# The final norm of a two-layer decoder trunk: its sum of squares by a full block of ones

## The chip, the cores and the metric

The kernel runs on one core of one Trainium2 chip. The metric is the device time of one execution in microseconds (us), as the median of three runs. TensorE (PE) multiplies matrices, VectorE (DVE), ScalarE (ACT) and GpSimd (POOL) work element by element, and SyncE (SP) issues most transfers. Each engine carries out its own instructions in a fixed order and waits on semaphores for the others.

## The reference

Two decoder layers over 512 tokens of width 1024: sparse attention and a dilated sliding window, each with heads into 256 memory tokens, and after each a SwiGLU of width 2816. The change touches only what comes last, the final norm:

```
def rms_norm(x, g):
    xf = x.astype(jnp.float32)
    y = xf * lax.rsqrt(jnp.mean(xf * xf, axis=-1, keepdims=True) + EPS)
    return (y * g.astype(jnp.float32)).astype(x.dtype)
...
    x = x + swiglu_ffn(rms_norm(x, norm_ffn), w_gate_up, w_down)
...
return rms_norm(x, final_norm)
```

## The kernel before, in words

The state x is kept transposed, as xT: eight tiles of 128 channels (partitions) by 512 tokens (columns). A sum over the channels of a token is thus a sum over partitions and over the eight tiles. Large products are done with weights and activations split into a high and a low float32r part, three matmuls for each; the norm's own small matmuls are plain float32, and each of those shows in the trace as two passes of weight load and matmul.

The last stage is `final`. It is called by `ffn(1)` for the last of the eight output tiles of the down projection (`down`, whose matmuls stand on lines 222 to 224 of `mm3`). By then tiles 0 to 6 of xT are done, and GpSimd adds up their squares in the tile `ssq` (`parts[0]`). ScalarE makes `xg`, the same tiles times the gains. The last tile is done in two halves of 256 tokens. For each half TensorE does 22 x 3 matmuls into one bank `psS`; VectorE adds the sum to xT (L1263), ScalarE squares the result into `t` (L1264), and `norm` finishes these 256 tokens.

`norm` sums the squares over partitions: for each block of 128 tokens a matmul has the squares as the stationary side and two columns of ones as the moving side, first with `ssq` (L1224), then with the square of the last tile (L1226). The result has tokens on partitions, one number each. ScalarE takes the root (L1227), VectorE the reciprocal (L1228), both of a single column. VectorE multiplies an identity matrix by that column (L1229), and a matmul of ones with these two diagonal blocks (L1232) spreads the numbers as a row over all partitions, into the bank `psacc`. ScalarE copies the row to SBUF (L1234), since GpSimd is given the copy; then six products on VectorE read `psacc` (L1241, L1243) and two on GpSimd the copy (L1239), and four transfers of two tiles each bring the output out (L1248). In the second half these go in turn by SyncE's and ScalarE's queues.

`norm` is a generator. For the first half it is created when its squares are; it runs up to its `yield` behind the first four of the 22 input tiles of the second half's down projection, and the rest behind the next four. TensorE carries out its instructions in the order in which the program issues them, so the first half's small matmuls stand between those of the second half's projection; the order of the other engines is set by the scheduler. For the second half nothing follows, and `norm` runs to its end.

Of the kernel before, what the change touches and what calls it, by code (L numbers as in the profile page):

```python
# [12 lines left out]
AF = mybir.ActivationFunctionType  # L13
ALU = mybir.AluOpType
AX = mybir.AxisListType

D = 1024
# [47 lines left out]
class _Trunk:  # L65
# [1137 lines left out]
    def final(self, ws, mh, ml):  # L1203

        nc, mm = self.nc, self.nc.tensor.matmul
        n = S // 2
        last = KT - 1
        add, parts = self.squares()
        for k in range(last):
            add(self.xT[:, k], 0, nc.gpsimd)  # L1210
        eps = self.cst.tile([128, 1], F32, name="eps")
        nc.vector.memset(eps, EPS)
        bigs = [self.big(name, F32).rearrange("p (k n) -> p k n", k=4) for name in ("xg", "xg", "y", "y")]
        xg, y = ([bigs[2 * a + k // 4][:, k % 4] for k in range(KT)] for a in range(2))
        for k in range(last):
            nc.scalar.activation(xg[k], self.xT[:, k], AF.Copy, scale=self.gains[:, 6, k:k + 1])

        def norm(b, sq):

            r, d = self.col("root", 2), self.tmp("raw")[:, :n]  # L1220
            blocks = [slice(i * 128, (i + 1) * 128) for i in range(2)]
            q = [self.psum("T")[:, :2] for _ in range(2)]
            for i in range(2):
                mm(q[i], parts[0][:, b][:, blocks[i]], self.ones[:, :2], start=True, stop=False)  # L1224
            for i in range(2):
                mm(q[i], sq[:, blocks[i]], self.ones[:, :2], start=False, stop=True)  # L1226
                nc.scalar.activation(r[:, i:i + 1], q[i][:, :1], AF.Sqrt, scale=1.0 / D, bias=eps)  # L1227
                nc.vector.reciprocal(r[:, i:i + 1], r[:, i:i + 1])  # L1228
                nc.vector.tensor_scalar(d[:, blocks[i]], self.ident, r[:, i:i + 1], None, op0=ALU.mult)  # L1229
            yield  # L1230
            p = self.psum("acc")[:, :n]
            mm(p, self.ones, d, start=True, stop=True)  # L1232
            row = self.tmp("raw")[:, :n]
            nc.scalar.copy(row, p)  # L1234
            done = set()
            for k in self.OUT_ORDER:
                o = y[k][:, b]
                if k in self.POOL_TILES:
                    nc.gpsimd.tensor_tensor(out=o, in0=xg[k][:, b], in1=row, op=ALU.mult)  # L1239
                elif k < last:  # L1240
                    nc.vector.tensor_tensor(out=o, in0=xg[k][:, b], in1=p, op=ALU.mult)  # L1241
                else:
                    nc.vector.scalar_tensor_tensor(o, self.xT[:, k, b], self.gains[:, 6, k:k + 1], p, op0=ALU.mult,  # L1243
                                                   op1=ALU.mult)
                done.add(k)
                j = k // 2 * 2
                if k ^ 1 in done:
                    (nc.sync, nc.scalar)[k // 2 % 2 * (b.start > 0)].dma_start(out[:, j:j + 2, b], bigs[2 + j // 4][:, j % 4:j % 4 + 2, b])  # L1248

        out = self.io["out"].rearrange("(k p) n -> p k n", p=128)  # L1250
        job = iter(())
        for h in range(2):
            b = slice(h * n, (h + 1) * n)
            p = self.psum("S")[:, :n]
            for w, k0, k1 in ws:
                for k in range(k0, k1, 4):
                    e = min(k + 4, k1)
                    c = slice((k - k0) * 128, (e - k0) * 128)
                    self.down(p, [m[:, c] for m in w], k, e, [m[:, b] for m in mh], [m[:, b] for m in ml])
                    next(job, None)  # L1260
            sq = self.tmp("t")[:, :n]
            with self.tc.high_priority():
                nc.vector.tensor_tensor(out=self.xT[:, last, b], in0=self.xT[:, last, b], in1=p, op=ALU.add)  # L1263
                nc.scalar.activation(sq, self.xT[:, last, b], AF.Square)  # L1264
            job = norm(b, sq)
        for _ in job:
            pass
# [116 lines left out]
```

## Time and profile before

| | us |
|---|---|
| median of three runs | 1240.79 |
| lowest and highest of them | 1238.21 and 1242.46 |
| the profiled execution | 1237.89 |
| its span, first to last instruction | 1236.0 |
| TensorE busy in it | 1196.5 |
| VectorE, ScalarE, GpSimd busy in it | 529.3, 484.1, 350.2 |

The span is what the trace covers; the profiled execution's time has 1.89 us more around it. Every row further down is of this one execution, and its times count from the start of the span. The final norm takes place in the last 18 us of it.

### The profile page before, as it was taken

The page shows a single profiled execution, that of the slowest core. Times are in us where ns is not written, and L with a number is a line of the kernel's source. Part 1 is how long each engine was busy: PE and PEld are TensorE (multiplying, and loading weights), DVE is VectorE, ACT ScalarE, POOL GpSimd, SP SyncE. Part 2 cuts the span into 40 slices and gives each one's busy share as a digit, 9 for nine tenths or more (in the row PEclk, how much of TensorE's full clock was granted, in tenths as well). Part 3 has the DMA queues.
Part 4 walks back from the last instruction along what each step waited for, and adds up shares of the span by engine and source line. Part 5 has one row for each costly group of instructions (what it writes and reads, how often), then busy time and mean ns, then how long its engine had stood idle before and what let it go on. Part 6 is the DMA issues. An engine that isn't in the chain of part 4 may idle for free.

```text
span 1236.0 us, 14342 instructions
## 1 busy us (share of the span) xinstructions
PE 1196.5 (97%) x5624; PEld 944.8 (76%) x5624; DVE 529.3 (43%) x1022; ACT 484.1 (39%) x852; POOL 350.2 (28%) x220
## 2 busy tenths in 40 slices
PE   9799899999999999999999999998999999999997
PEld 5367576578788888888888778886788888888886
DVE  4769724547433333332224543559433333331112
ACT  3663584424423323222222776545323223222222
POOL 0444453245222122212222323324322122211222
PEclk9899999999999999999999999999999999999999
DMA  5313103102322222222233121211222222222221
GB/s 189 130 38 132 57 35 95 59 34 92 110 76 99 102 102 103 79 96 94 94 115 113 58 69 34 83 55 69 91 82 100 103 103 101 77 87 94 94 94 69
DMA packets 29185, 108.36 MB, mean 88 GB/s; under 512 B 2494, under 2 KB 11582, under 8 KB 20670
## 3 DMA queue, kind: packets, MB, share of 16 engines
q1 hardware_dynamic: 28574, 106.93, 24.6%
q8 instruction: 44, 0.72, 0.2%
q10 hardware_dynamic: 544, 0.52, 0.1%
q14 instruction: 23, 0.19, 0.0%
HBM read 104.43 MB, written 3.01 MB: 87 GB/s over the span
## 4 chain that ended last, share of the span: by engine, by line
PE 77%; DVE 10%; DMA 4%; issue 4%; ACT 3%; POOL 2%; SPq 0%; DVEq 0%; POOLq 0%; ACTq 0%
PE psS L249 5%; PE psS L247 5%; PE psS L248 5%; PE psT L249 3%; PE psT L247 3%; PE psT L248 3%; PE psacc L249 3%; PE psacc L247 3%; PE psacc L248 3%; PE psacc L222 3%; PE psacc L224 3%; PE psacc L223 3%; PE psS L222 3%; PE psS L224 3%; PE psS L223 3%
## 5 line engine op out<-in xcount | busy, mean ns | idle before, releaser
L51 POOL TENSOR_TENSOR wl<-wf,wh 128x1024 fp32r<-128x1024 f32 x92 | 222.7, 2422 | 618.9 <-ACT wh L48 567.4
L48 ACT CAST wh<-wf 128x1024 fp32r<-128x1024 f32 (+1 forms) x163 | 167.4, 1030 | 505.4 <-issue 156.1
L51 DVE TENSOR_TENSOR wl<-wf,wh 128x1024 fp32r<-128x1024 f32 (+1 forms) x84 | 99.4, 1184 | 80.0 <-ACT wh L48 80.0
L249 PE MATMUL psS<-xh,wl 128*128 128x512 f32 x272 | 106.9, 393 | 0.0
L247 PE MATMUL psS<-xh,wh 128*128 128x512 f32 x272 | 106.5, 392 | 0.0
L248 PE MATMUL psS<-xl,wh 128*128 128x512 f32 x272 | 106.1, 390 | 0.0
L247 PE MATMUL psacc<-xh,wh 128*128 128x512 f32 x192 | 75.5, 393 | 0.6 <-DVE xT L653 0.6
L247 PE MATMUL psT<-xh,wh 128*128 128x512 f32 x192 | 75.5, 393 | 0.0
L249 PE MATMUL psT<-xh,wl 128*128 128x512 f32 x192 | 75.5, 393 | 0.0
L249 PE MATMUL psacc<-xh,wl 128*128 128x512 f32 x192 | 75.5, 393 | 0.0
L248 PE MATMUL psT<-xl,wh 128*128 128x512 f32 x192 | 74.9, 390 | 0.0
L248 PE MATMUL psacc<-xl,wh 128*128 128x512 f32 x192 | 74.9, 390 | 0.0
L316 POOL TENSOR_TENSOR ssq<-ssq,t 128x512 f32<-128x512 f32 (+1 forms) x31 | 41.0, 1322 | 96.6 <-ACT t L306 61.1
L248 PEld LDWEIGHTS psS<-xl,wh 128*128 128x128 f32 x272 | 51.1, 188 | 11.6
L249 PEld LDWEIGHTS psS<-xh,wl 128*128 128x128 f32 x272 | 51.1, 188 | 11.1
L247 PEld LDWEIGHTS psS<-xh,wh 128*128 128x128 f32 x272 | 51.1, 188 | 10.7
L235 PE MATMUL psacc<-xh,wh 128*128 128x512 f32 x136 | 58.1, 428 | 0.0
L668 DVE TENSOR_TENSOR raw<-psacc,R 128x512 f32<-128x512 f32 x22 | 15.2, 691 | 96.9 <-PE psacc L249 96.9
L237 PE MATMUL psacc<-xh,wl 128*128 128x512 f32 x136 | 54.1, 398 | 0.0
L236 PE MATMUL psacc<-xl,wh 128*128 128x512 f32 x136 | 54.0, 397 | 0.0
L653 DVE TENSOR_TENSOR xT<-xT,psacc 128x512 f32<-128x512 f32 x44 | 30.0, 683 | 39.0 <-PE psacc L224 38.9
L247 PEld LDWEIGHTS psacc<-xh,wh 128*128 128x128 f32 x192 | 36.1, 188 | 8.7 <-issue 1.2
(320 smaller groups left out, 2628.8 us busy)
## 6 DMA issues: line engine op xcount, KB each, us to landing
wf<-in_gu SPq DMA_DIRECT2D x44, 1024.0 KB
wf<-in_dn SPq DMA_DIRECT2D x16, 1024.0 KB
wf<-in_in SPq DMA_DIRECT2D x12, 1024.0 KB
wf<-in_dn SPq DMA_DIRECT2D x16, 384.0 KB
wf<-in_v SPq DMA_DIRECT2D x3, 1024.0 KB
wf<-in_in SPq DMA_DIRECT2D x5, 512.0 KB
xT<-in_x SPq DMA_DIRECT2D x8, 256.0 KB
wf<-in_mk SPq DMA_DIRECT2D x2, 1024.0 KB
```

The lines of the kernel that those rows point to most:

```text
L48: nc.scalar.copy(hi, src)
L51: lo_engine.tensor_tensor(out=lo, in0=src, in1=hi.bitcast(F32), op=ALU.subtract)
L222: mm(out, wh[k], xh[k], start=first and k == 0, stop=False)
L223: mm(out, wh[k], xl[k], start=False, stop=False)
L224: mm(out, wl[k], xh[k], start=False, stop=last and k == n - 1)
L235: mm(out, wh[:, s], xh[k], start=k == 0, stop=False)
L236: mm(out, wh[:, s], xl[k], start=False, stop=False)
L237: mm(out, wl[:, s], xh[k], start=False, stop=k == KT - 1)
L247: mm(out, wh[:, s], xh[k], start=k == 0, stop=False)
L248: mm(out, wh[:, s], xl[k], start=False, stop=False)
L249: mm(out, wl[:, s], xh[k], start=False, stop=k == KT - 1)
L316: engine.tensor_tensor(out=parts[part], in0=parts[part], in1=sq, op=ALU.add)
```

## The change

The sum over partitions is done the other way round: the block of ones is the stationary side, and the squares are the moving side. The result of the two matmuls is at once a row of 256 tokens, the same on all 128 partitions, in one bank `psT`. Root and reciprocal then work on 128x256 elements each; the reciprocal is written to the bank `psacc`, from which everything goes on as before. The single columns, the diagonal blocks and the spreading matmul are gone. From here on line numbers of the changed kernel are 3 to 5 lower than those of the same statements before.

```
         def norm(b, sq):
 
-            r, d = self.col("root", 2), self.tmp("raw")[:, :n]
-            blocks = [slice(i * 128, (i + 1) * 128) for i in range(2)]
-            q = [self.psum("T")[:, :2] for _ in range(2)]
-            for i in range(2):
-                mm(q[i], parts[0][:, b][:, blocks[i]], self.ones[:, :2], start=True, stop=False)
-            for i in range(2):
-                mm(q[i], sq[:, blocks[i]], self.ones[:, :2], start=False, stop=True)
-                nc.scalar.activation(r[:, i:i + 1], q[i][:, :1], AF.Sqrt, scale=1.0 / D, bias=eps)
-                nc.vector.reciprocal(r[:, i:i + 1], r[:, i:i + 1])
-                nc.vector.tensor_scalar(d[:, blocks[i]], self.ident, r[:, i:i + 1], None, op0=ALU.mult)
+            q = self.psum("T")[:, :n]
+            mm(q, self.ones, parts[0][:, b], start=True, stop=False)
+            mm(q, self.ones, sq, start=False, stop=True)
+            root = self.tmp("raw")[:, :n]
+            nc.scalar.activation(root, q, AF.Sqrt, scale=1.0 / D, bias=eps)
+            p = self.psum("acc")[:, :n]
+            nc.vector.reciprocal(p, root)
             yield
-            p = self.psum("acc")[:, :n]
-            mm(p, self.ones, d, start=True, stop=True)
             row = self.tmp("raw")[:, :n]
             nc.scalar.copy(row, p)
             done = set()
```

On TensorE, in the first half's norm, behind the first four input tiles of the second half's projection (a row is line, operation, what it writes and reads; `psT` is the bank of the sums, `ssq` and `t` are the squares):

```order
 L224 MATMUL psS<-midh,wl 128x256
-L1224 MATMUL psT<-ones,ssq 128x2 x2
-L1226 MATMUL psT<-ones,t 128x2 x2
+L1221 MATMUL psT<-ssq,ones 128x256
+L1222 MATMUL psT<-t,ones 128x256
 L222 MATMUL psS<-midh,wh 128x256
```

Four products of two columns have become two of 256, at the same place in the stream; the spreading product that followed twelve matmuls later in the stream is gone as well.

On TensorE, at the end of the program, in the second half's norm:

```order
 L223 MATMUL psS<-ml,wh 128x256
 L224 MATMUL psS<-mh,wl 128x256
-L1224 MATMUL psT<-ones,ssq 128x2 x2
-L1226 MATMUL psT<-ones,t 128x2 x2
-L1232 MATMUL psacc<-raw,ones 128x256
-L1380 UNCONDITIONAL_BRANCH
+L1221 MATMUL psT<-ssq,ones 128x256
+L1222 MATMUL psT<-t,ones 128x256
+L1375 UNCONDITIONAL_BRANCH
```

The product with `t` is now the last of the program; before, the spreading product out of the diagonal blocks (`raw`) was.

On VectorE, the changed kernel's two norms with the adds to xT that stand ahead of each (L1258):

```order
L1258 TENSOR_TENSOR xT<-xT,psS 128x256
L1226 RECIPROCAL psacc<-raw 128x256
L1236 TENSOR_TENSOR y<-xg,psacc 128x256 x5
L1238 SCALAR_TENSOR_TENSOR y<-xT,gains,psacc 128x256
L1258 TENSOR_TENSOR xT<-xT,psS 128x256
L1226 RECIPROCAL psacc<-raw 128x256
```

One reciprocal of 128x256 stands where two of one column and two diagonal blocks stood, and the add for the second half stays behind the first half's six products.

## Rows read from the trace of the kernel before

**Rows 1.** The page's first lines: span, and each engine's busy time.

```profile
span 1236.0 us, 14342 instructions
...
PE 1196.5 (97%) x5624; PEld 944.8 (76%) x5624; DVE 529.3 (43%) x1022; ACT 484.1 (39%) x852; POOL 350.2 (28%) x220
```

**Rows 2.** Chain of waits, first half's norm: start us, us, what.

```profile
1218.67 0.34 PE psT L1224 x4
1219.01 0.45 PE psT L1226 x4
1219.46 0.23 PE psS L222
...
1220.98 0.43 PE psacc L1232 x2
1221.41 0.12 PE psS L222
```

**Rows 3.** Chain of waits, second half's norm.

```profile
1226.42 0.02 issue
1226.45 0.43 DVE xT L1263
...
1227.39 0.04 issue
1227.43 0.40 PE psT L1226 x2
1227.83 0.02 issue
1227.85 0.49 ACT root L1227 x2
...
1228.37 0.16 DVE root L1228
1228.53 0.39 DVE raw L1229 x2
...
1228.97 0.71 PE psacc L1232 x2
1229.68 0.02 issue
1229.71 0.38 ACT raw L1234
```

**Rows 4.** Timeline of ScalarE and VectorE, first half: start, duration, instruction, idle time before.

```profile
1218.25 1.28 ACT L1227 ACT_TABLE_LOAD   x1
...
1221.86 1.74 DVE L1241 TENSOR_TENSOR y<-xg,psacc 128x256 f32<-128x256 f32 x5 [1.32 <-ACT raw L1234]
1223.52 0.47 DVE L1243 SCALAR_TENSOR_TENSOR y<-xT,gains,psacc 128x256 f32<-128x256 f32 x1
```

**Rows 5.** Groups by line and form, ScalarE: busy us, mean ns, idle us before.

```profile
L585 ACT ACTIVATE raw<-psS,nm 128x256 f32<-128x256 f32 x32 | 14.8, 474 | 10.1 <-DVE nm L581 10.0
L417 ACT ACTIVATE vm<-psacc,rs_keep 128x256 f32<-128x256 f32 x4 | 1.9, 474 | 12.1 <-PE psacc L215 12.0
L1234 ACT COPY raw<-psacc 128x256 f32<-128x256 f32 x2 | 0.7, 372 | 2.9 <-PE psacc L1232 2.9
```

**Rows 6.** Groups by line and form, VectorE.

```profile
L1241 DVE TENSOR_TENSOR y<-xg,psacc 128x256 f32<-128x256 f32 x10 | 3.5, 414 | 2.5 <-ACT raw L1234 2.5
L498 DVE RECIPROCAL den<-den 128x8 f32<-128x8 f32 x10 | 2.0, 198 | 8.7 <-ACT raw L622 7.3 <-ACT raw L585 1.5
L965 DVE TENSOR_TENSOR mf<-me,mm 128x8 f32<-128x8 f32 x4 | 0.5, 163 | 0.1
L263 DVE TENSOR_TENSOR rs_q<-rs_keep 128x2 f32<-128x2 f32 x3 | 0.5, 157 | 0.1
L962 DVE RECIPROCAL mm<-mm 128x8 f32<-128x8 f32 x2 | 0.4, 201 | 0.0
```

**Rows 7.** Line 1228 alone: duration ns as min/median/max, starts, form.

```profile
L1228 DVE RECIPROCAL root<-root x4: 162/164/166, 1219.8 to 1228.4; 128x1 f32<-128x1 f32 x4
```

## The prediction

> **What bounds the kernel now.** I read the page's table of engines first, then the chain of waits over the last 20 us, then the groups by line and form for the operations that come and go, and last the timeline for what stands beside the chain.
>
> The table of engines has TensorE busy for 97% of the span [rows 1], so the kernel is a stream of matmuls with a short tail. The change touches the stream at two places, both in the last 18 us. In the first half of the final norm its matmuls stand between those of the second half's down projection, and the chain runs over them [rows 2]: what they take there is paid in full. In the second half no matmul is left to hide anything: the chain goes through each step, VectorE, ScalarE, TensorE, ScalarE, VectorE, TensorE, ScalarE, with 0.02 to 0.04 us from one engine to the next [rows 3]. From the copy of the row (L1234, 1229.71) on nothing changes: the same six products on VectorE, two on GpSimd, the same four transfers, to 1236.0. I therefore count two terms, the stream's time in the first half, and the time from the end of the last square (L1264) to the start of that copy in the second.
>
> **First half.** Removed are four products of two columns (eight passes in the trace, since each float32 matmul shows as two) and the spreading product (two passes). They take 0.34 + 0.45 us, the matmul behind them takes 0.23 instead of the 0.12 of its neighbours, and the spreading product takes 0.43 [rows 2]: 0.34 + 0.45 + 0.11 + 0.43 = 1.33 us. Added are two products of ones with 256 moving columns. That is the shape of the spreading product, which cost 0.43 in the stream and left the next matmul at 0.12 [rows 2], so 2 x 0.43 = 0.86. The term is 0.86 - 1.33 = -0.47 us. If each cost what the spreading product costs when it comes out of a wait, 0.71 [rows 3], it would be 1.42 - 1.33 = +0.09; a larger gain than 0.47 has no row. I take -0.47, since the stream is not interrupted.
>
> The rest of the first half is off the chain. The second product ends at 1218.67 + 0.86 = 1219.53. ScalarE loads its table from 1218.25 for 1.28, also to 1219.53 [rows 4], so the root is not later than that load allowed already. With the root at 0.47 and a reciprocal of D the copy ends and VectorE's products begin at 1219.53 + 0.02 + 0.47 + 0.02 + D + 0.04 + 0.38 + 0.02 = 1220.48 + D, and are through 2.13 us later (before: 1221.86 to 1223.99, [rows 4]), at 1222.61 + D. Behind them VectorE has the last add to xT, which before begins at 1226.45 and now, with the stream 0.47 earlier, wants to begin at 1225.98. So the first half hides its reciprocal up to D = 3.37 us; beyond, each microsecond of D is paid a second time.
>
> **Second half.** Before, from the start of the two-column products with the last square (1227.43) to the start of the copy (1229.71) it is 2.28 us: 0.40 TensorE, 0.49 two roots of one column, 0.16 that is left of the reciprocals, 0.39 that is left of the two diagonal blocks, 0.71 spreading product, and 0.13 in handing over [rows 3]. After:
> - The product with the last square has 256 columns and comes out of a wait, as the spreading product did: 0.71. The one with the sum of the other squares needs nothing late; TensorE has from 1226.42 to 1227.43 for it [rows 3], and it takes 0.43 to 0.71, so it is hidden with 0.3 us to spare.
> - One root of 128x256 out of PSUM with a column as its bias: the activations of that size out of PSUM that take a column cost 0.474, the plain copy 0.372 [rows 5]. I take 0.47; the other end is 0.10 less.
> - One reciprocal of 128x256, VectorE, D.
> - Handing over 0.02 + 0.02 + 0.04 = 0.08.
>
> Together 1.26 + D, so the term is D - 1.02. Neither diagonal block nor spreading product remains. The copy's reader on VectorE waits for ScalarE as it did. That the reciprocal writes to PSUM has no row on VectorE; reading PSUM there costs nothing that shows (0.414 for the products out of PSUM, [rows 6]), and I add nothing.
>
> **The reciprocal** decides the sign. No row has it wider than 8 columns. Other VectorE operations barely grow at that width: 157 ns for 2 columns, 163 for 8, 414 for 256, about 1.0 ns a column. The reciprocal grows from 164 ns for 1 column to 198 and 201 for 8 [rows 6, 7]: (201 - 164) / 7 = 5.3 ns a column, five times as much. Three readings:
> - The growth is start-up and the rate that of a product: D = 0.41.
> - The growth is the rate: D = 0.164 + 255 x 5.3 ns = 1.52.
> - The single column's excess over an ordinary narrow operation is the rate. An ordinary one would take 157 - 2 = 155 ns without any column, and the reciprocal of one column takes 162 to 164 [rows 7], so 7 to 9 ns: D = 0.155 + 256 x 7 ns = 1.95, or x 9 ns = 2.46.
>
> I take 1.52: it is the only one that rests on a difference within one operation, and it lies between.
>
> As a page of the Trainium skill has it ("VectorE: DVE Perf Modes", section "First, the fixed hardware budget"), a reciprocal is an iterative divide with a repeat count of 8. At eight clocks of the page's 0.96 GHz a column that gives, as an estimate from that page, 2.13 us above the start, D near 2.3, and the sum would be about +0.8 us instead of what follows here. The trace agrees that a column costs several times a product's, but with 5.3 ns rather than 8.3; no run here shows a wide one.
>
> **The sum.** -0.47 + (1.52 - 1.02) = +0.03 us. The profiled execution took 1237.89 us (its span of 1236.0 and 1.89 around it), so the changed kernel's profile would have 1237.92. The median of the three runs shown is 1240.79, 2.90 above that execution, with runs from 1238.21 to 1242.46; the difference carries over, and the forecast is 1240.8 us. What TensorE saves in the stream, VectorE gives back in the tail.
>
> **The rivals.**
> 1. The reciprocal runs at the rate of a product (D = 0.41). For it: a product of that form needs 414 ns, and one could read the 37 ns as start-up. Against it: the single column already has the start-up. Tail -0.61, sum -1.08: 1239.7 us. Chance 0.15.
> 2. The reciprocal takes 7 to 9 ns a column (D = 1.95 to 2.46), the last reading above. For it: the 7 to 9 ns of the first column. Against it: seven further columns add 37 ns, and not 49 to 63. Sum -0.47 + 0.93 to 1.44 = +0.5 to +1.0: 1241.5 us at its middle, slower but too little to be told. Chance 0.27. The case of the Trainium skill's page above lies in this rival's span.
> 3. Slower by more than can be mistaken: the reciprocal is so slow that it is paid in both halves. The place is VectorE's queue, in which the first half's products stand ahead of the last add to xT. From D = 3.37 us on the sum is -0.47 + (D - 1.02) + (D - 3.37) = 2D - 4.86; it reaches +3.7 us at D = 4.28, 16 ns a column: 1244.5 us. Nothing in the rows grows so fast. Chance 0.03.
> 4. The stream gains nothing in the first half, because each wide product stalls it as one out of a wait does (0.71): sum +0.59, 1241.4 us. Against it is the 0.43 measured in that same stream. Chance 0.05.
>
> That the change doesn't do what it says I exclude: the order has neither the diagonal blocks nor the spreading product.
>
> **How the numbers follow.** The forecast has 0.50, the rivals 0.15, 0.27, 0.03 and 0.05. What a measurement of this kernel can tell from no change is about 0.3%, 3.7 us. All cases but the third lie inside that, between -1.2 (rival 1 with the shorter root) and +1.5 (rivals 2 and 4 together). Beyond that there is only the runs' own spread, -2.6 to +1.7 about their median, which a median of three seldom uses up. Range: 1240.8 less 1.2 and 2.4 is 1237.2; plus 1.0 and 2.2 is 1244.0. The likeliest case's own range is the spread alone, 1238.4 to 1243.0. Faster by over 0.3%: 0.03 (spread on top of rival 1). Slower by over 0.3%: 0.05 (rival 3, and spread on rival 2). Within: 0.92.
>
> **What would show it.** In the profile after: one reciprocal per half, of 128x256, and its duration, 1.5 us by the forecast, 0.4 and 2.0 to 2.5 by the first two rivals; one root per half at 0.47; on the chain in the stream two products of 0.43 and no third; in the tail some 2.8 us instead of 2.28 from the product with the last square to the copy; the last add to xT still begun by TensorE and not behind VectorE's products. The prediction is wrong if the reciprocal is outside 1.1 to 1.95 us, if the stream pays over 0.6 for a wide product, or if the time from the copy to the end is not the 6.3 us of before.

## The result and the profile after

The changed kernel takes 1254.24 us (median of 4 runs, 1251.63 to 1257.41) against 1240.47 us before (4 runs, one more than the prediction had): ratio 1.0108, with a 95% interval of 1.0078 to 1.0137. It is slower by 13.8 us, where 1240.8 and at most 1244.0 were forecast.

The norm itself looks almost as forecast. These are pieces of the changed kernel's chain of waits (start us, us, what): first the first half's norm in the stream, which answers to [rows 2], then the second half's in the tail, which answers to [rows 3]:

```profile
1238.09 0.43 PE psT L1221 x2
1238.52 0.43 PE psT L1222 x2
...
1246.22 0.04 issue
1246.26 0.71 PE psT L1222 x2
1246.98 0.02 issue
1247.00 0.48 ACT raw L1224
1247.48 0.02 issue
1247.51 1.77 DVE psacc L1226
1249.28 0.02 issue
1249.30 0.38 ACT raw L1229
```

Two products of 0.43 stand in the stream, and no third. The tail from the product with the last square to the copy is 1249.30 - 1246.26 = 3.04 us instead of 2.28, so 0.76 longer, with a root of 0.48 and a reciprocal of 1.77. Of the groups by line and form on VectorE, two answer to [rows 6]:

```profile
L1226 DVE RECIPROCAL psacc<-raw 128x256 f32<-128x256 f32 x2 | 3.5, 1761 | 4.1 <-ACT raw L1224 4.1
L498 DVE RECIPROCAL den<-den 128x8 f32<-128x8 f32 x10 | 2.0, 198 | 8.7 <-ACT raw L622 7.3 <-ACT raw L585 1.5
```

A reciprocal of 256 columns takes 1761 ns, so (1761 - 164) / 255 = 6.3 ns for each column beyond the one-column form of [rows 7].

None of this is 13.8 us. The loss is in the part of the program that nobody touched. The page's first lines, which answer to [rows 1], show TensorE with 18 us more of busy time and fewer instructions:

```profile
span 1255.6 us, 14311 instructions
...
PE 1214.6 (97%) x5612; PEld 947.0 (75%) x5612; DVE 532.3 (42%) x1016; ACT 484.4 (39%) x850; POOL 348.4 (28%) x220
```

The busy time of two stretches (us, then us and number of instructions of PE, PEld, DVE, ACT and POOL, then the granted clock, the DMA share and GB/s), of the kernel before:

```profile
0.00:100.00 100.00, 87.19 (x343) 54.24 (x344) 65.28 (x152) 57.26 (x108) 32.08 (x32) 0.95 0.37 123
900.00:1000.00 100.00, 100.00 (x438) 82.04 (x438) 34.93 (x46) 30.11 (x37) 21.66 (x9) 1.00 0.27 95
```

And of the changed kernel:

```profile
0.00:100.00 100.00, 86.42 (x317) 53.31 (x318) 59.56 (x134) 53.58 (x102) 28.07 (x29) 0.90 0.34 113
900.00:1000.00 100.00, 100.00 (x430) 80.56 (x429) 33.45 (x46) 28.82 (x36) 21.57 (x9) 1.00 0.27 95
```

From 900 to 1000 us both are in the second layer's gate and input products, TensorE is busy throughout at the full granted clock, and before it begins 438 matmuls there, after 430: one every 228 ns, and one every 233. The same instructions in the same order take 2% longer each. (Split matmuls are the three float32r matmuls that make up one large product.) When VectorE's and ScalarE's instructions are followed through both traces, the changed kernel is 5.9 us behind at 100 us, 6.1 at 200, 9.5 at 500, 13.7 at 900 and 19.7 at 1210: after the start it loses in the stretches of split matmuls and hardly elsewhere. The 5.9 us of the first 100 us are a matter of the single execution: there the granted clock was 0.90 on the mean in this one (20.5 us at 1.2 GHz, the lower of its two levels) and 0.95 in the one before (10.2 us), and among the kernels further down 0.88 to 0.90 and 0.95 to 0.97 both occur, at good addresses and at bad ones. The other 13.8 us agree with the difference of the medians.

What differs is where the tiles lie. The old norm took its roots from `self.col("root", 2)`, a tag of four buffers, each of which takes 32 bytes a partition; the change removes the tag, and what is allocated behind it moves 128 bytes down. From the two programs' tables of allocations (first byte in the partition, and remainder by 256):

```
                        before            changed
xh, xl, midh, midl      48640 ...    0    48640 ...    0    (2048 columns)
mh, ml, oh, ol          137152 ... 192    137152 ... 192    (512 columns)
root                    185920 ...        gone
wf (two buffers)        186048     192    185920      64
wh (three buffers)      202432     192    202304      64
wl (three buffers)      214720     192    214592      64
```

wh and wl hold the weights. In the split matmuls of 512 columns they are the stationary side and tiles of the other two groups the moving side; on lines 441 to 443, at 256 columns, it is the other way round.

### The profile page after: what moved, and what is told of

The parts are those of the page before. It is cut to its first block, busy times and chain, and to the rows that moved or that the text cites. A ratio compares the mean times of both kernels' runs of the same rounds, so it can differ in the third digit from the quotient of the medians.

```text
span 1255.6 us, 14311 instructions
## 1 busy us (share of the span) xinstructions
PE 1214.6 (97%) x5612; PEld 947.0 (75%) x5612; DVE 532.3 (42%) x1016; ACT 484.4 (39%) x850; POOL 348.4 (28%) x220
## 4 chain that ended last, share of the span: by engine, by line
PE 79%; DVE 10%; issue 4%; DMA 3%; ACT 3%; POOL 1%; SPq 0%; DVEq 0%; POOLq 0%; ACTq 0%
PE psS L249 5%; PE psS L247 5%; PE psS L248 5%; PE psT L248 3%; PE psT L247 3%; PE psT L249 3%; PE psacc L222 3%; PE psacc L247 3%; PE psacc L249 3%; PE psacc L248 3%; PE psacc L223 3%; PE psacc L224 3%; PE psS L223 3%; PE psS L224 3%; PE psS L222 3%
## 5 line engine op out<-in xcount | busy, mean ns | idle before, releaser
L653 DVE TENSOR_TENSOR xT<-xT,psacc 128x512 f32<-128x512 f32 x44 | 30.1, 686 | 40.0 <-PE psacc L224 39.7
```

## The experiments

In what follows "distance" is the remainder by 256 of the weights' address less that of the moving side's. "Apart" is the mean time from the start of a split matmul of 512 columns to the start of the next one, worked out from the start times in the trace without gaps over 400 ns. It is taken over those output tiles of both layers' down products that go into `psS`, as the mean over the three lines 222 to 224, with 72 matmuls on each line for midh and midl (2048-column tiles) and 60 for mh and ml (512-column tiles). All of them run at the full granted clock.

| kernel | ratio to before (95%) | distance, apart: midh, midl | distance, apart: mh, ml |
|---|---|---|---|
| before | 1 | 192, 229.3 ns | 0, 228.2 ns |
| changed | 1.0108 (1.0078 to 1.0137) | 64, 233.3 | 128, 232.2 |
| e1_pad128 | 1.0011 (0.9986 to 1.0036) | 192, 229.3 | 0, 228.2 |
| e2_norm_before | 1.0114 (1.0080 to 1.0148) | 64, 233.3 | 128, 232.4 |
| e3_pad64 | 1.0096 (1.0060 to 1.0131) | 128, 232.6 | 192, 229.4 |
| e4_pad192 | 0.9971 (0.9952 to 0.9989) | 0, 227.1 | 64, 233.3 |
| e5_pad256 | 1.0113 (1.0088 to 1.0137) | 64, 233.3 | 128, 232.4 |
| e6_all_up_128 | 1.0115 (1.0090 to 1.0139) | 64, 233.3 | 128, 232.4 |
| e7_all_alike | 0.9958 (0.9939 to 0.9977) | 0, 226.7 | 0, 226.7 |
| e8_all_alike_old_norm | 0.9935 (0.9912 to 0.9958) | 0, 226.7 | 0, 226.7 |
| e9_pad160 | 1.0117 (1.0073 to 1.0161) | 224, 233.3 | 32, 233.3 |
| e10_pad224 | 1.0127 (1.0078 to 1.0176) | 32, 233.4 | 96, 234.1 |

**e1_pad128: the addresses back, the new norm kept.** In the changed kernel's `final`:

```
+        nc.vector.memset(self.act.tile([128, 32], F32, tag="pad", bufs=1, name="pad")[:, :1], 0.0)
```

The memset is one more instruction on VectorE (in e11 there are two); beside it, the order of instructions in the trace is that of the changed kernel on every engine. This holds for all kernels with such a pad (e1, e3, e4, e5, e7, e9, e10, e11); e2, e6 and e8 need none.

> The changed kernel with an unused tile of 128 bytes a partition (of which one column is set to zero) in the place where the old norm's column tiles stood, so that the weight tiles wf, wh and wl lie at the addresses of before. Theory A (the addresses): the change took 128 bytes out of SBUF ahead of the weight tiles, and the float32r matmuls that read those tiles now start 233 ns apart where it was 226 to 232; with the addresses back the stream is back, 1240 to 1242 us, ratio to before 0.999 to 1.002. Theory B (the new norm itself, or work that it displaces): nothing changes, ratio 1.008 to 1.014.

Measured: 1243.87 us against 1241.16 in the same session, ratio 1.0011 (0.9986 to 1.0036), and the starts are as far apart as before, to 0.1 ns. One stretch of its busy times, as above, with 439 matmuls:

```profile
900.00:1000.00 100.00, 100.00 (x439) 82.05 (x438) 34.31 (x45) 29.30 (x36) 22.77 (x10) 1.00 0.27 95
```

Theory A holds; what the new norm by itself costs or gains is too little to be told from the times.

**e2_norm_before: the old norm kept, the addresses of the changed kernel.** In the kernel before:

```
-            r, d = self.col("root", 2), self.tmp("raw")[:, :n]
+            r, d = self.col("rs_y", 4)[:, :2], self.tmp("raw")[:, :n]
```

> The kernel before with its norm, but the two reciprocal roots stand in a column tile that the kernel has anyway (rs_y), so that the weight tiles wf, wh and wl move 128 bytes down as in the changed kernel. Theory A (the addresses): as slow as the changed kernel, 1252 to 1256 us, ratio 1.008 to 1.014, starts of split matmuls 233 ns apart. Theory B (the norm): as before, ratio 0.997 to 1.003.

Measured: 1256.76 us, ratio 1.0114 (1.0080 to 1.0148). The order of instructions is that of before on every engine, only a tile's name is another, and the kernel is as slow as the changed one. Two stretches of its busy times:

```profile
0.00:100.00 100.00, 86.94 (x346) 55.38 (x347) 66.26 (x155) 57.42 (x109) 32.85 (x32) 0.95 0.38 124
900.00:1000.00 100.00, 100.00 (x430) 80.55 (x430) 33.93 (x45) 28.57 (x36) 21.45 (x9) 1.00 0.27 95
```

It is 430 matmuls again, although the granted clock of the first 100 us is 0.95 as before. So the loss belongs to the moved weight tiles, and the norm has no part in it that can be told.

**e3_pad64 and e4_pad192: other places.** As e1 with a pad of 64 and of 192 bytes (16 and 48 columns).

> The changed kernel with 64 unused bytes ahead of the weight tiles, so that they begin 64 bytes above the changed kernel's place and 64 below the place before. Theory A leaves open how the stream depends on the address: if it counts in 64 bytes and repeats after 256, this is a third value, anywhere from 1235 to 1256 us, with the starts of split matmuls apart in proportion (1 ns for about 3.5 us). Theory B: ratio 1.008 to 1.014 as for the changed kernel.

> The changed kernel with 192 unused bytes ahead of the weight tiles, so that they begin at a multiple of 256 bytes. Theory A: a value of its own, 1235 to 1256 us; if only 128 bytes mattered it would be that of 64. Theory B: ratio 1.008 to 1.014.

Measured: 1254.31 us, ratio 1.0096 (1.0060 to 1.0131), and 1237.51 us, ratio 0.9971 (0.9952 to 0.9989). Theory B falls with the second, which is quicker than before. Within e4 the midh products are at 227.1 ns and the mh products, with the same weights, at 233.3: so the weights' address alone doesn't decide. The same two numbers speak against a rival that no run was made for, that the casts, differences and transfers that fill the moved tiles get in TensorE's way: these are the same for both groups of products.

**e5_pad256: the same remainder, 256 bytes higher.** As e1 with 256 bytes.

> The changed kernel with 256 unused bytes ahead of the weight tiles, which then begin 256 bytes higher, at the same remainder of 256 as in the changed kernel (64). Theory A1 (the remainder of the address by 256 counts): as slow as the changed kernel, ratio to before 1.008 to 1.014, split matmuls 233 ns apart. Theory A2 (the weights have to lie high enough, at 186048 or more, whatever the remainder; the two kernels so far at or over it were quick, the three below it slow): as quick as with 128 or 192 bytes, ratio 0.995 to 1.003.

Measured: 1253.71 us, ratio 1.0113 (1.0088 to 1.0137). The height doesn't count (A2 falls); 256 bytes on, all is as it was.

**e6_all_up_128: weights and activations moved together.** In the changed kernel, ahead of all working tiles:

```
-        eps = self.cst.tile([128, 1], F32, name="eps")
+        eps = self.cst.tile([128, 33], F32, name="eps")[:, :1]
```

> The changed kernel with 128 unused bytes ahead of all working tiles (the tile that holds eps is made 132 bytes wide), so that activations and weights move together: the weights lie where they lay before (remainder 192), the activations 128 bytes higher, and the distance from one to the other is the changed kernel's. Theory A3 (the distance between weights and moving side by 256 counts): as slow as the changed kernel, ratio 1.008 to 1.014. Theory A1 (the weights' own remainder): as quick as before, 0.998 to 1.004.

Measured: 1253.67 us, ratio 1.0115 (1.0090 to 1.0139):

```profile
900.00:1000.00 100.00, 100.00 (x430) 80.56 (x429) 33.75 (x45) 28.55 (x36) 21.66 (x9) 1.00 0.27 95
```

The weights are where they were before, and it is slow: A1 falls. With e4, what counts is the distance between a matmul's two operands.

**e7_all_alike and e8_all_alike_old_norm: distance 0 everywhere.** Both widen a column tile by 64 bytes in all; e7 is the changed kernel, which also has a pad of 128 bytes as in e1, e8 the kernel before:

```
-        yi = self.act.tile([128, 4], I32, tag="rs_i", bufs=2, name="rs_i")[:, :n]
+        yi = self.act.tile([128, 16], I32, tag="rs_i", bufs=2, name="rs_i")[:, :n]
```

> The changed kernel with all operands of the split matmuls at a multiple of 256 bytes: a column tile of integers is widened so that the 512-column tiles (mh, ml, oh, ol) move from remainder 192 to 0, and 128 unused bytes stand ahead of the weights. Theory A3: by the runs so far the large tiles at distance 0 from the weights cost 227 ns a matmul and the 512-column tiles at distance 0 some 228; so no group of 512 columns is at 233 any more; some 2200 matmuls of the gate and input products gain 2.4 ns over before and 540 of the down product 2.3, 6.5 us together: 1234 us, ratio 0.992 to 0.996, quicker than with 192 bytes (0.997). Theory A1: the weights' remainder is that of the kernel with 192 bytes, so its ratio, 0.997, comes again.

> The kernel before with its own norm, and all operands of the split matmuls at a multiple of 256 bytes, as in e7_all_alike. Beside that kernel it shows what the norm itself is worth on the same addresses. By the trace of the changed kernel the new norm's tail is 0.76 us longer (reciprocal 1.76 us) and its share of the stream some 0.4 us shorter: this one should be quicker by 0.3 us, which is less than can be told; ratio to before 0.992 to 0.996. If the norm had a cost of its own of microseconds, the two would lie apart by that.

Measured: 1235.42 us, ratio 0.9958 (0.9939 to 0.9977), and 1231.08 us, ratio 0.9935 (0.9912 to 0.9958). Both beat both kernels. The same stretch of e7 has 443 matmuls, one every 226 ns:

```profile
900.00:1000.00 100.00, 100.00 (x443) 82.81 (x442) 34.74 (x46) 29.95 (x37) 21.53 (x9) 1.00 0.29 99
```

e7's interval still reaches e4's 0.9971, so its time alone doesn't confirm A3 over A1; its mh products, at 226.7 ns instead of e4's 233.3 with the weights in the same place, do. Between e7 and e8 the times show no clear difference: the medians are 4.3 us apart, but the intervals overlap, and the runs go from 1230.1 to 1238.7 us in e7 and from 1229.2 to 1238.2 in e8. On the trace the norm alone can be compared on equal addresses, from the add of the last full tile (L653) to the end of the span. It is 1229.3 - 1202.22 = 27.08 us in e7 and 1227.5 - 1200.73 = 26.77 in e8; 26.85 in e1 and 26.55 before; 26.49 in the changed kernel and 26.34 in e2. The new norm costs 0.15 to 0.31 us more.

**e9_pad160 and e10_pad224: steps of 32 bytes.** As e1 with pads of 160 and 224 bytes (40 and 56 columns).

> The changed kernel with 160 unused bytes ahead of the weight tiles: their remainder by 256 is 224, so the distance weights minus activations is 224 to the large tiles and 32 to the 512-column tiles. By the distance (A3), and if it is a smooth matter, the large tiles lie between distance 192 (227 to 230 ns) and 0 (227), some 228, and the 512-column tiles between 0 (227) and 64 (233), some 230: ratio 0.996 to 1.000. If it counts in steps of 64 bytes, 32 is like 0 or like 64, 227 or 233 ns, and 224 like 192 or like 0.

> The changed kernel with 224 unused bytes ahead of the weight tiles: remainder 32, so the distance is 32 to the large tiles and 96 to the 512-column tiles. By the distance (A3), smooth: large tiles some 230 ns, 512-column tiles some 233: ratio 1.002 to 1.008. In steps of 64: large tiles 227 or 233.

Measured: 1257.12 us, ratio 1.0117 (1.0073 to 1.0161), and 1256.82 us, ratio 1.0127 (1.0078 to 1.0176), both slower than either had been given. It is not smooth: 32 bytes off in either direction costs what 64 does (233.3 ns), and only 0 and, part of the way, 192 are clearly better.

**e11_low_weights_64: whose weights.** e7 with wl alone moved:

```
+        if not hasattr(self, "gap"):
+            self.gap = self.wp.tile([128, 16], F32, tag="gap", bufs=1, name="gap")
+            self.nc.vector.memset(self.gap[:, :1], 0.0)
         wl = self.wp.tile([128, 1024], F32R, tag="wl", bufs=3, name="wl")[:, :n]
```

> The kernel with all split operands at a multiple of 256, but with the tiles wl alone moved 64 bytes up. Three matmuls follow one another: wh by xh (or midh, mh), wh by xl, wl by xh. Theory B1: the extra time comes from the weight load that runs beside a matmul, of the next matmul's weights; wl is loaded beside the one with xl, so the starts after the matmuls of lines 248, 223 and 236 go to 233 ns and the other two of each three stay at 227. Theory B2: it comes from the matmul's own weights; then those of lines 249, 224 and 237 go to 233 and the others stay. Either way a third of the loss: ratio 0.998 to 1.002.

Measured: 1248.45 us, ratio 1.0040 (1.0018 to 1.0061), more than either theory gave. By the ratios it is 0.8% over e7 (1.0040 / 0.9958), where the changed kernel is 1.5% over it, so over half the loss and not a third. The starts behind the matmuls that use wl (line 249 before; midh alike) are 235.8 ns apart, those behind the other two of each three 228.3 to 229.2, where e7 has 226.3 to 227.8 for all. The stretch from 900 to 1000 us has 435 matmuls, between e7's 443 and the changed kernel's 430:

```profile
900.00:1000.00 100.00, 100.00 (x435) 81.26 (x434) 34.48 (x46) 29.47 (x37) 21.68 (x9) 1.00 0.27 95
```

As B2 had it, most of the time is lost behind the matmul whose own weights are off, and 1 to 3 ns come on behind its neighbours; why the neighbours lose is open. Nor does it say where in the hardware the two operands meet, since a weight load runs beside the matmul ahead of its own: before, the load for line 224 and the matmul of line 223 both start at 1199.89 us.

## Why the prediction was wrong, point by point

**The step that failed is the first one.** The prediction said that the change touches the stream at two places, both in the last 18 us, and read each removed line as instructions. One removed line also took a tile away: `self.col("root", 2)`. Four buffers of 32 bytes went, the weight tiles moved 128 bytes, and the split matmuls of 512 columns came some 4 ns later one after another. By the kinds of lines, 2232 matmuls of the gate and input products (lines 247 to 249) went from a mean of 229.1 to 233.5 ns, 9.8 us; 540 with midh or midl from 229.3 to 233.3, 2.2 us; 450 with mh or ml from 228.2 to 232.2, 1.8 us. That is 13.8 us, as much as was measured, without the smaller groups. Neither a term nor a rival had it: all four rivals were about the norm, and the range was theirs. The prediction's signs of being wrong looked at the norm alone too, and none of them came up: the reciprocal took 1.76 us, a wide product 0.43, and from the copy to the end it was 1255.6 - 1249.30 = 6.3 us.

**First half: right.** Forecast -0.47 us of stream. On equal addresses, from the first half's add to xT to the second's, it was 9.15 us before (1217.30 to 1226.45) and 8.70 in e1 (1225.79 to 1234.49): -0.45. Each wide product cost 0.43; rival 4 falls. In the changed kernel that last add begins behind TensorE and not behind VectorE's products, as forecast (start us, us, instruction, and in brackets the idle time before it and what ended it); rival 3 falls.

```profile
1243.38 0.47 DVE L1238 SCALAR_TENSOR_TENSOR y<-xT,gains,psacc 128x256 f32<-128x256 f32 x1
1245.28 0.42 DVE L1258 TENSOR_TENSOR xT<-xT,psS 128x256 f32<-128x256 f32 x1 [1.43 <-PE psS L224]
```

**Second half: the mechanism right, one term too small.** Forecast +0.50, measured +0.76; the 0.71 came as put, and the root, at 0.48 for 0.47, and the hand-overs within 0.02. The reciprocal was put at 1.52 us and took 1.76, 6.3 ns a column instead of 5.3, between the forecast and rival 2. The reading by the growth from 1 to 8 columns was low; that the one-column form's 164 ns hold part of a floor would explain it, but no run tried it. The Trainium skill's repeat count of 8 ("VectorE: DVE Perf Modes", section "First, the fixed hardware budget"), taken as eight clocks a column, had given an estimate near 2.3 us; the 1.76 measured is less, and the measurement decides. That a reciprocal grows several times as fast as a product was right (6.3 ns a column against some 1.0), and rival 1 falls.

**The sum of the norm** was forecast at +0.03, and is +0.15 to +0.31 by the traces on equal addresses; e1's ratio holds it at no change. So the argument about the norm would have stood if the tiles had stayed where they were.

**What stays open.** That the distance by 256 between the stationary and the moving operand decides is shown by e4, e5, e6 and e7; why it does is not shown by any run. Nor is it explained why 192 lies part of the way, and why mh and ml were at 228.2 ns at distance 0 before and at 226.7 in e7.

## What to carry to other kernels

A change that adds or drops a tile moves all tiles that are allocated behind it, so compare the tables of allocations of both programs before you count instructions. When matmuls that nobody touched run at another rate at the same granted clock, suspect addresses: put a pad of the lost size back, and take it out of the old kernel. Here operands of 512-column float32r matmuls at the same remainder by 256 were worth 0.4 to 0.7% over the kernel as it was tuned, and the price of being off was 1%.

## What the runs showed of the hardware

- Split (float32r) matmuls of 128x128 by 512 columns start 226.7 to 228.2 ns apart when both operands have the same remainder by 256, 229.3 to 229.4 at a distance of 192, and 232 to 234 at 32, 64, 96, 128 and 224 (32, 96 and 224 by e9 and e10 alone).
- At 256 columns the order is reversed: means of 119.8 and 120.0 ns at distance 0 (midl and ml in e7), 114.3 and 113.9 at 64 (midl in the changed kernel, ml in e4). Lines 441 to 443, where the weights are the moving side, go the same way: medians of 114 to 116 ns before (distance 64) and 120 in e7 (0). So in this kernel the best place depends on the length of the moving side; few of its split matmuls are so short.
- The plain float32 matmuls show no such effect: 429 ns for 512 columns (median, line 207), before and after, although their weights wf moved by the same 128 bytes. The transposes of 128 columns (line 469) have 109 before and in e6, where one of their two operands moved by 128 bytes.
- A reciprocal on VectorE takes 164 ns for 1 column (before), 198 for 8 and 1761 for 256 (changed).
